# Memory keys and values from plain float32 products of the weights as loaded, the values with the memory tokens on the partitions

## Chip, cores and metric

The kernel runs on one core of one Trainium2 chip. The metric is the device time of one execution in microseconds (us), taken as the median of several runs. Engines are named as in the profile: PE is TensorE's matmul, PEld its weight load, DVE is VectorE, ACT is ScalarE, POOL is GpSimd, SP is SyncE, whose queue (SPq) issues the transfers.

## The reference, cut to what matters

One layer of a streaming encoder over T = 1088 rows (1024 prompt frames and 64 sample frames) with D = 1024 channels. Besides the big projection `h @ w_in` of the frames it needs keys and values of 256 memory tokens, which are outputs of their own and are read later by the cross-attention:

```python
def memory_kv(mem, g_mem, w_mem_kv):          # mem (1, 256, 1024), w_mem_kv (1024, 2048)
    kv = rmsnorm(mem, g_mem) @ w_mem_kv
    k, v = jnp.split(kv, 2, axis=-1)          # each (1, 256, 1024) -> 4 heads of 256
    return (k.reshape(b, N_MEM, N_MEM_HEADS, MEM_HEAD_DIM), v.reshape(b, N_MEM, N_MEM_HEADS, MEM_HEAD_DIM))
...
mem_k, mem_v = memory_kv(mem_prompt, g_mem[l], w_mem_kv[l])
...
q_sb, k_sb, v_sb, u_sg, v_sg, q_mem, z_gate = jnp.split(h @ w_in, cuts, axis=-1)
...
o_mem = cross_attend(q_mem, mem_k, mem_v)
```

## The kernel before, in words

All large products are made in float32r with each operand split in two: `split` (line 241) writes a rounded high part by a copy (on ACT, or on DVE where `lighter`, line 236, finds DVE's clock cheaper) and the rest by a subtraction on DVE; `mm3` (line 249) adds the products high by high, high by low and low by high. So one product of full precision is three matmul instructions, and each weight block of 128 x 512 elements costs a copy and a subtraction (`wsplit`, line 460).

The program is a list of steps in a fixed order. The first 16 (`n_mem`) belong to the memory keys and values: for each of 4 heads and for keys (`kv` = 0) and values (`kv` = 1) a pair of steps m = 0, 1 from `memkv_pair` (line 807) through `conv_pair` (line 591). A pair reads two raw weight tiles of 512 KB (`raw_load`, line 449), splits each into two `whl` tiles, and in each step adds up eight chunks of 128 input channels for 128 output channels (on the partitions) by 256 memory tokens (the columns) in one PSUM tile `pb`. ACT copies that into `mkT`. When both steps of a pair are done, `fin` (line 819) turns the pair round by four transposes on PE, DVE copies it to `mko` (the rows to be stored), and `split` writes `mhl` (of `mkT` for keys, of `mko` for values); two stores follow. Then come 36 Strassen units of seven steps each for `w_in` (`strassen_unit`, line 476), which need split forms (`XhB11a`, `XlT2b` and so on) of the normalised, transposed and scaled frames.

Those forms are made while the memory steps run. Each tile of frames `xt` is loaded (at most four ahead, `X_AHEAD`), squared and summed on ACT, scaled, transposed on PE in two groups of four, multiplied by its gain into `bt` (`gain`, line 714, DVE or four ACT instructions), and then five groups of subtractions and splits (`form_stages`, line 726) make seven forms of it. This work is put into the instruction streams by a planner that runs while the program is built: it keeps an estimated clock for each engine (`Clocks`, line 94), and between products (`breathe`, `fill`, lines 356 and 365) emits stages whose inputs it takes to be ready, as long as DVE and ACT are no more than `BACK` us (6 here, `BACKLOG_MEM`) ahead of PE. Each engine then works through its own instructions in that order. Its estimate for a float32r product of 256 columns is 0.107 us, and for a plain float32 product 0.0017 us for each column, 0.435 us for 256.

Weights are fetched by counting weight tiles ("wops"): `get_wop(i)` (line 398) forms the tiles up to `LA` = 2 beyond i and issues raw loads whose first wop lies up to `LA` + `RA` = 4 beyond i. The tiles share 40 slots in SBUF (`arena`, tag "s"), those of 2 KB share 11 (tag "u"). All loads and stores go through SP's queue in order. The input of the memory steps is prepared ahead of step 0 by `fm` (line 2057): the memory tokens are scaled, transposed, multiplied by `g_mem` and split into `MH["h"]` and `MH["l"]`.

Of the kernel before, what the change touches and what calls it, by code (L numbers as in the profile page):

```python
# [9 lines left out]
F32 = mybir.dt.float32  # L10
F32R = mybir.dt.float32r
# [4 lines left out]
P = 128  # L16
# [77 lines left out]
class Clocks:  # L94
# [43 lines left out]
    def at(self, *tiles):  # L138
        return max([self.wrote.get(x.tensor.name, (0,))[0] for x in tiles], default=0) + self.LATENCY
# [16 lines left out]
def encoder_layer(  # L156
# [14 lines left out]
    clock, at = clocks.t, clocks.at  # L171
    nc = Engines(tc.nc, clocks)
# [10 lines left out]
    def nm(s):  # L183
        cnt[0] += 1
        return f"{s}_{cnt[0]}"

    def A(shape, dt=F32, s="a"):
        return arena.tile(shape, dt, tag="s", name=nm(s), bufs=NSLOT)

    def U(shape, dt=F32, s="u"):  # L190
        return arena.tile(shape, dt, tag="u", name=nm(s), bufs=NSMALL)
# [3 lines left out]
    def PB():  # L195
        t = ps.tile([P, 1024], F32, tag="b", name=nm("pb"), bufs=3)
        banks["b"] = banks["b"][-2:] + [t]
        return t

    def PT():  # L200
        t = ps.tile([P, 512], F32, tag="t", name=nm("pt"), bufs=2)
        banks["t"] = banks["t"][-1:] + [t]
        return t

    def psum_free(tag, n=1):

        h = banks[tag]
        return clocks.done(h[n - 1]) if len(h) == (3 if tag == "b" else 2) else 0
# [27 lines left out]
    def lighter(src, n, cost_dve):  # L236

        t = at(src)
        return max(clock["dve"], t) + cost_dve < max(clock["act"], t) + 0.1 + 0.00084 * n

    def split(src, hi, lo):
        n = math.prod(list(src.shape)[1:])
        if src.space == bass.MemoryType.SB and lighter(src, n, DVE_BIAS + 0.07 + 0.00057 * n):
            nc.vector.tensor_copy(hi, src)
        else:
            act(hi, src)
        sub(lo, src, f32(hi))
# [6 lines left out]
    def tp(out, in_):  # L254
        n = in_.shape[0]
        nc.tensor.transpose(out, in_, ident[:n, :n])
# [7 lines left out]
    c_gmem, c_gpre, c_gffn, c_lng, c_lnb = [cols[:, 8 * i:8 * i + 8] for i in range(5)]  # L264
# [46 lines left out]
    def stream(*stages):  # L311
        st = list(stages)
        streams.append(st)
        return st
# [41 lines left out]
    def breathe():  # L356

        tick()
        while clock["dve"] < clock["pe"] + BACK[0] and clock["act"] < clock["pe"] + BACK[0]:
            st = ready(0)  # L360
            if st is None:
                break
            go(st)

    def fill(t):

        while clock["pe"] < t - 0.2:
            st = ready(t - 0.2)
            if st is None:
                break  # L370
            go(st)
# [16 lines left out]
    raws, wops, steps = [], [], []  # L388
# [6 lines left out]
    def get_raw(i):  # L395
        return raw_t[i]
# [33 lines left out]
    def wop(fn, *rs):  # L430

        wops.append(fn)
        for r in rs:
            first_wop.setdefault(r, len(wops) - 1)
            last_wop[r] = len(wops) - 1
        return len(wops) - 1
# [12 lines left out]
    def raw_load(srcs, nk):  # L449

        def f():
            r = A([P, nk, 256], F32, "raw")
            w = 256 // len(srcs)
            for i, s in enumerate(srcs):
                load(r[:, :, i * w:(i + 1) * w], s.rearrange("(k p) m -> p k m", p=P))
            return r
        raws.append(f)
        return len(raws) - 1
# [132 lines left out]
    def conv_pair(parts, xf, halves, evac, post=None, pre=None, kept=None, first=True, last=True):  # L591

        rs = [raw_load(srcs, nk) for srcs, nk in parts] if first else []

        def mk(i, m):
            nk = parts[i][1]

            def f():  # L600
                return wsplit(get_raw(rs[i])[:, :, m * P:(m + 1) * P], nk)
            return wop(f, rs[i])
        for m in range(2):
            ws = [mk(i, m) for i in range(len(parts))] if first else []
            K = sum(nk for _, nk in parts)

            def f(tiles, m=m, K=K):
                if not first:
                    tiles = kept[m]
                    ahead(AH_OUT[0] < 0)  # L610
                    AH_OUT[0] -= 1
                if kept is not None:
                    kept[m] = None if last else tiles
                if pre:
                    pre(m)
                for hi, chunks in enumerate(halves):
                    fill(psum_free("b"))
                    pt = PB()
                    for (t, s, out) in chunks:
                        k = 0  # L620
                        for i, (_, nk) in enumerate(parts):
                            for kk in range(nk):
                                xh, xl = xf(k, t, s)
                                if kk == 0:
                                    fill(at(tiles[i], xh, xl))
                                mm3(out(pt), tiles[i][:, 0, kk, :], tiles[i][:, 1, kk, :], xh, xl,
                                    k == 0, k == K - 1)
                                k += 1
                            if i < len(parts) - 1 or (t, s) != chunks[-1][:2]:
                                breathe()  # L630
                    evac(m, hi, pt)
                    breathe()
                    if post:
                        post(m, hi)
            steps.append((ws, f))

    def cols_of(a, b):
        return lambda pt: pt[:, a:b]
# [75 lines left out]
    def gain(out, src, g):  # L714

        n = src.shape[2]
        t = at(src)
        if max(clock["dve"], t) + 0.07 + 0.0042 * n < max(clock["act"], t) + 4 * (0.1 + 0.00084 * n) + G_BIAS:
            mul(out, src, g.unsqueeze(2).to_broadcast([P, 4, n]))
        else:  # L720
            for k in range(4):
                act(out[:, k], src[:, k], scale=g[:, k:k + 1])
# [82 lines left out]
    MH = {}  # L805

    def memkv_pair(h, kv):
        col = kv * D + h * 256
        parts = [([w_mem_kv[0, kh * 512:(kh + 1) * 512, col:col + 256]], 4) for kh in range(2)]
        st = {}  # L810

        def evac(m, hi, pt):
            if m == 0:
                st["t"] = U([P, 2, 256], F32, "mkT")
            act(st["t"][:, m, :], pt[:, :256])
            if m == 1:
                stream(("pe", lambda: max(at(st["t"]), psum_free("t")), fin))

        def fin():
            t = st["t"]  # L820
            pt = PT().rearrange("p (m d) -> p m d", m=2)
            for m in range(2):
                for dt in range(2):
                    tp(pt[:, m, dt * P:(dt + 1) * P], t[:, dt, m * P:(m + 1) * P])
            o = U([P, 2, 256], F32, "mko")
            nc.vector.tensor_copy(o, pt)
            dst = mem_v_prompt if kv else mem_k_prompt

            hl = A([P, 2, 2, 256], F32R, "mhl")
            split(o if kv else t, hl[:, 0], hl[:, 1])  # L830

            def put():
                store(dst[0, 0, :, h, :].rearrange("(m p) d -> p m d", p=P), o)
                store((memv if kv else memk)[h], f32(hl).rearrange("p s m d -> p (s m d)"))
            later(0, put, (o, hl))
        conv_pair(parts, lambda k, t, s: (MH["h"][k // 4][:, k % 4, :], MH["l"][k // 4][:, k % 4, :]),
                  [[(0, "a", cols_of(0, 256))]], evac)

    for h in range(4):
        for kv in range(2):  # L840
# [1205 lines left out]
    r = 0  # L2046
# [2 lines left out]
        load(vecs[r:r + n, :], v.rearrange("o (r p) -> (o r) p", p=P))  # L2049
        r += n  # L2050
    get_wop0()
    MH["h"] = [A([P, 4, 256], F32R, "memh") for _ in range(2)]
    MH["l"] = [A([P, 4, 256], F32R, "meml") for _ in range(2)]
    for j in range(2):
        d = {}

        def fm(j=j, d=d):
            bt = A([P, 8, P], F32, "bt")
            for k, p in tr4(d):
                gain(bt[:, k], p, c_gmem[:, k])  # L2060
            for q in range(2):
                split(bt[:, 4 * q:4 * q + 4], MH["h"][q][:, :, j * P:(j + 1) * P],
                      MH["l"][q][:, :, j * P:(j + 1) * P])
            READY["mem"] = READY.get("mem", 0) + 1
        stream(rms_stage(lambda j=j: mt[j], d), scale_stage(lambda d=d: d if "r" in d else None),
               ("pe", lambda d=d: max(at(d["x"]), psum_free("t")) if "cols" in READY else None, fm))
    until(lambda: not any(st[0][0] == "act" for st in streams))
    pt = PT()
# [7 lines left out]
    for n, i in enumerate([0, 1, 2, 3, 8, 4, 5, 6, 7]):  # L2076
        def ld(i=i):
            H[i] = load_tile(i, x_prompt[0], x_sample[0])
        d = {}
        e1, n1, a = rms_stage(lambda i=i: H[i], d)  # L2080
# [122 lines left out]
```

## Time and profile before

| | |
|---|---|
| median of 3 runs | 2271.82 us (2271.15 to 2273.85) |
| the profiled execution | 2273.61 us |
| its span, first to last instruction | 2271.9 us |
| mean granted TensorE clock | 0.993 |
| PE busy | 2217.8 us (98%), 16465 instructions |
| DVE busy | 1545.8 us (68%) |
| ACT busy | 760.8 us (33%) |

The span is what the trace shows; the execution's own time is 1.7 us more, and that execution was 1.8 us over the median. Busy PE counts the time from a matmul's start to its modelled end, and consecutive matmuls overlap, so the start times of a run of matmuls tell more than their durations. The lines of the views carry the line number 84 throughout, since every operation is recorded by one helper: instructions are told apart by the names of their tiles.

### The profile page before, as it was taken

To read this page: it belongs to the slowest core of one execution; us is meant where nothing else is said; L and a number is where in the kernel's file an instruction comes from. 1 tells how busy PE (TensorE), PEld (TensorE's weight loads), DVE (VectorE), ACT (ScalarE), POOL (GpSimd) and SP (SyncE) were. 2 spreads that over 40 slices of the span, in tenths; PEclk is the share of its full clock that TensorE was granted. 3 is DMA by queue.
4 is the path that set the end of the run, shared out by engine and by line. 5 is a ranking of instruction groups with operands and counts; after the bars stand their busy time and mean duration, and the time that the engine had idled before them with its cause. 6 is when DMAs were issued, how large, how long until landed. Compare 5 with 4: busy or idle time off the path is not lost. (4 is left out here: it accounts for less than half of the span.)

```text
span 2271.9 us, 40720 instructions
## 1 busy us (share of the span) xinstructions
PE 2217.8 (98%) x16465; PEld 2146.1 (94%) x16465; DVE 1545.8 (68%) x2451; ACT 760.8 (33%) x1403; POOL 61.5 (3%) x144
## 2 busy tenths in 40 slices
PE   7899999999999999999999999998999999999998
PEld 6799999999999999889999999997999999998876
DVE  7955688865777776788734353468677677675677
ACT  8442222232212232566522021354112112134353
POOL 1000000000000000011000000000000000000000
PEclk9999999999999999999999999998999999999999
DMA  6523355775476658886835252132232233257235
GB/s 209 186 87 105 125 208 199 235 224 161 167 263 215 221 188 267 295 295 219 278 127 164 88 165 68 55 105 85 86 118 92 75 118 95 72 180 261 84 112 185
DMA packets 288367, 368.27 MB, mean 162 GB/s; under 512 B 20628, under 2 KB 220404, under 8 KB 288180
## 3 DMA queue, kind: packets, MB, share of 16 engines
q1 hardware_dynamic: 288180, 365.67, 48.6%
q8 instruction: 130, 2.13, 0.4%
q14 instruction: 57, 0.47, 0.1%
HBM read 234.86 MB, written 131.80 MB: 161 GB/s over the span
## 5 line engine op out<-in xcount | busy, mean ns | idle before, releaser
L84 ACT ACTIVATE whl<-raw 128x512 fp32r<-128x512 f32 x256 | 157.8, 634 | 523.5 <-PE pb L84 203.8
L84 DVE TENSOR_TENSOR c<-pb,u 128x544 f32<-128x544 f32 (+2 forms) x236 | 168.3, 713 | 228.3 <-PE pb L84 215.6
L84 PE MATMUL pb<-fop,fop 128*128 128x512 f32 x924 | 219.3, 390 | 1.8 <-DVE p L84 1.6
L84 PEld LDWEIGHTS pb<-fop,fop 128*128 128x128 f32 x924 | 173.0, 188 | 40.5 <-DVE p L84 2.4
L84 DVE TENSOR_TENSOR whl<-raw,whl 128x512 fp32r<-128x512 f32 x270 | 180.5, 683 | 13.9 <-ACT whl L84 13.3
L84 DVE TENSOR_TENSOR u<-pb,u 128x544 f32<-128x544 f32 (+2 forms) x177 | 125.7, 710 | 58.7 <-PE pb L84 57.9
L84 DVE TENSOR_TENSOR whl<-u,whl 128x512 fp32r<-128x512 f32 x232 | 160.1, 690 | 6.1
L84 PE MATMUL pb<-XhB11a,whl 128*128 128x288 f32 x592 | 130.8, 296 | 0.7 <-ACT whl L84 0.5
L84 PE MATMUL pb<-XhB21a,whl 128*128 128x288 f32 x592 | 130.8, 296 | 0.0
L84 PE MATMUL pb<-XhB22a,whl 128*128 128x288 f32 x592 | 130.1, 295 | 0.0
L84 PE MATMUL pb<-XhB11b,whl 128*128 128x256 f32 x592 | 120.0, 286 | 0.0
L84 ACT ACTIVATE c<-c 128x1088 f32<-128x1088 f32 x38 | 42.4, 1116 | 229.8 <-DVE c L84 229.8
L84 PE MATMUL pb<-XhB21b,whl 128*128 128x256 f32 x592 | 119.1, 284 | 0.0
L84 PE MATMUL pb<-XhB22b,whl 128*128 128x256 f32 x592 | 118.6, 283 | 0.0
L84 PE MATMUL pb<-XhT2a,whl 128*128 128x288 f32 x464 | 104.4, 300 | 2.3 <-DVE whl L84 0.4
L84 PE MATMUL pb<-Xrh,whl 128*128 128x288 f32 (+1 forms) x512 | 101.4, 293 | 1.9 <-ACT ysq L84 1.9
L84 PE MATMUL pb<-XhT1a,whl 128*128 128x288 f32 x464 | 102.0, 295 | 0.9 <-DVE sgo L84 0.9
L84 PE MATMUL pb<-XhT3a,whl 128*128 128x288 f32 x464 | 102.2, 296 | 0.0
L84 PE MATMUL pb<-XhT4a,whl 128*128 128x288 f32 x464 | 102.0, 295 | 0.0
L84 PEld LDWEIGHTS pb<-XhB11a,whl 128*128 128x128 f32 x592 | 99.0, 188 | 1.1 <-ACT whl L84 0.7
L84 PEld LDWEIGHTS pb<-XhB21a,whl 128*128 128x128 f32 x592 | 99.0, 188 | 0.0
L84 PEld LDWEIGHTS pb<-XhB22a,whl 128*128 128x128 f32 x592 | 99.0, 188 | 0.0
(327 smaller groups left out, 6226.6 us busy)
## 6 DMA issues: line engine op xcount, KB each, us to landing
raw<-in_w_in_dram SPq DMA_DIRECT2D x72, 512.0 KB
raw<-in_w_ffn_in_dram SPq DMA_DIRECT2D x88, 256.0 KB
gsc<-c SPq DMA_DIRECT2D x24, 544.0 KB
grow<-gsc SPq DMA_DIRECT2D x24, 544.0 KB
raw<-in_w_branch_dram SPq DMA_DIRECT2D x24, 512.0 KB
fS<-fsum SPq DMA_DIRECT2D x44, 256.0 KB
fw<-in_w_ffn_out_dram SPq DMA_DIRECT2D x44, 256.0 KB
fa<-fS SPq DMA_DIRECT2D x44, 256.0 KB
```

What stands on the lines that cost most here:

```text
L84: r = fn(*a, **k)
```

## The change

The weights of the memory steps are no longer split. A step takes the raw tiles as they were loaded and makes eight plain float32 matmuls with the float32 tokens `MH["x"]`, which `fm` now writes directly by `gain`. For keys the weights are the stationary operand as before; for values the tokens are, so that the result has the tokens on its partitions, and `fin` needs neither transposes nor the copy to `mko` for them. The weight tiles counted by `wop` are now the raw tiles themselves, two for a pair, both with step m = 0.

```diff
     def memkv_pair(h, kv):
         col = kv * D + h * 256
-        parts = [([w_mem_kv[0, kh * 512:(kh + 1) * 512, col:col + 256]], 4) for kh in range(2)]
+        rs = [raw_load([w_mem_kv[0, kh * 512:(kh + 1) * 512, col:col + 256]], 4) for kh in range(2)]
         st = {}
+        def step(m):
+            def f(tiles):
+                w = tiles or st["w"]
+                st["w"] = w
+                fill(psum_free("b"))
+                pt = PB()
+                for kh in range(2):
+                    fill(at(w[kh], MH["x"][kh]))
+                    for k in range(4):
+                        products(pt, w[kh], MH["x"][kh], m, k, kh == k == 0, kh == 1 and k == 3)
+                    breathe()
+                evac(m, 0, pt)
+                breathe()
+                if m == 1:
+                    del st["w"]
+            steps.append(([wop(lambda r=r: get_raw(r), r) for r in rs] if m == 0 else [], f))
+
+        def products(pt, w, x, m, k, start, stop):
+            a, b = (x, w) if kv else (w, x)
+            nc.tensor.matmul(pt[:, :256], lhsT=a[:, k, m * P:(m + 1) * P], rhs=b[:, k, :], start=start, stop=stop)
 
         def evac(m, hi, pt):
...
             if m == 1:
-                stream(("pe", lambda: max(at(st["t"]), psum_free("t")), fin))
+                stream(("dve", lambda: at(st["t"]), fin) if kv else
+                       ("pe", lambda: max(at(st["t"]), psum_free("t")), fin))
 
         def fin():
-            t = st["t"]
-            pt = PT().rearrange("p (m d) -> p m d", m=2)
-            for m in range(2):
-                for dt in range(2):
-                    tp(pt[:, m, dt * P:(dt + 1) * P], t[:, dt, m * P:(m + 1) * P])
-            o = U([P, 2, 256], F32, "mko")
-            nc.vector.tensor_copy(o, pt)
+            t = o = st["t"]
+            if not kv:
+                pt = PT().rearrange("p (m d) -> p m d", m=2)
+                for m in range(2):
+                    for dt in range(2):
+                        tp(pt[:, m, dt * P:(dt + 1) * P], t[:, dt, m * P:(m + 1) * P])
+                o = U([P, 2, 256], F32, "mko")
+                nc.vector.tensor_copy(o, pt)
             dst = mem_v_prompt if kv else mem_k_prompt
...
-        conv_pair(parts, lambda k, t, s: (MH["h"][k // 4][:, k % 4, :], MH["l"][k // 4][:, k % 4, :]),
-                  [[(0, "a", cols_of(0, 256))]], evac)
+        for m in range(2):
+            step(m)
...
-    MH["h"] = [A([P, 4, 256], F32R, "memh") for _ in range(2)]
-    MH["l"] = [A([P, 4, 256], F32R, "meml") for _ in range(2)]
+    MH["x"] = [A([P, 4, 256], F32, "memx") for _ in range(2)]
     for j in range(2):
         d = {}
 
         def fm(j=j, d=d):
-            bt = A([P, 8, P], F32, "bt")
             for k, p in tr4(d):
-                gain(bt[:, k], p, c_gmem[:, k])
-            for q in range(2):
-                split(bt[:, 4 * q:4 * q + 4], MH["h"][q][:, :, j * P:(j + 1) * P],
-                      MH["l"][q][:, :, j * P:(j + 1) * P])
+                gain(MH["x"][k.start // 4][:, :, j * P:(j + 1) * P], p, c_gmem[:, k])
```

## Rows read from the trace of the kernel before

**Rows 1.** The page: busy tenths of PE in 40 equal slices of the span.
```profile
PE   7899999999999999999999999998999999999998
```

**Rows 2.** Busy time by stretch: PE, PEld, DVE, ACT, POOL; then granted clock, DMA share, GB/s.
```profile
0.00:94.00 94.00, 70.82 (x503) 66.19 (x503) 75.67 (x147) 66.57 (x157) 8.54 (x17) 0.96 0.63 203
14.00:40.00 26.00, 24.39 (x179) 23.42 (x180) 18.57 (x36) 23.80 (x53) 4.67 (x7) 1.00 0.89 286
40.00:94.00 54.00, 42.27 (x310) 39.53 (x309) 51.03 (x98) 35.24 (x94) 1.59 (x2) 0.94 0.48 154
110.00:2271.00 2161.00, 2131.53 (x15847) 2065.06 (x15846) 1455.42 (x2280) 688.79 (x1235) 52.94 (x127) 0.99 0.49 160
```

**Rows 3.** Waits of PE, 14 to 94 us: total, times, longest.
```profile
PE pb L84 <- DVE whl L84: 8.0, 8, 2.5
PE pt L84 <- ACT bt L84: 4.2, 6, 1.3
PE pb L84 <- ACT whl L84: 2.9, 2, 2.4
```

**Rows 4.** PE in order of time, memory steps: start, duration, what, count.
```profile
14.17 0.58 PE L84 MATMUL pb<-memh,whl 128*128 128x256 f32 x1 [2.41 <-ACT whl L84]
...
17.75 0.41 PE L84 MATMUL pb<-meml,whl 128*128 128x256 f32 x1
...
19.87 0.40 PE L84 MATMUL pb<-memh,whl 128*128 128x256 f32 x2
...
24.98 0.28 PE L84 MATMUL pb<-meml,whl 128*128 128x256 f32 x1
...
27.13 0.28 PE L84 MATMUL pb<-meml,whl 128*128 128x256 f32 x1
...
27.37 1.04 PE L84 MATMUL pt<-ident,xt 128*128 128x128 f32 x8
28.16 0.36 PE L84 MATMUL pb<-memh,whl 128*128 128x256 f32 x1
28.36 0.28 PE L84 MATMUL pb<-meml,whl 128*128 128x256 f32 x1
...
93.61 0.40 PE L84 MATMUL pb<-XhB11a,whl 128*128 128x288 f32 x1 [0.46 <-ACT whl L84]
```

**Rows 5.** By tile, a memory load, plain products: durations min/median/max ns, first and last start.
```profile
L84 PEld LDWEIGHTS pb<-memh,whl x256: 186/192/337, 14.2 to 92.8; 128*128 128x128 f32 x128
...
L84 PEld LDWEIGHTS pb<-wsT,vct x128: 186/192/192, 641.2 to 693.6; 128*128 128x128 f32 x128
...
L84 PE MATMUL pb<-ys,sel x4: 590/592/592, 2171.3 to 2172.6; 128*128 128x512 f32 x4
```

**Rows 6.** PE in order of time around two of those products.
```profile
641.34 1.95 PE L84 MATMUL pb<-wsT,vct 128*128 128x128 f32 x16
643.22 0.43 PE L84 MATMUL pt<-wsT,vct 64*128 64x64 f32 x2
```

**Rows 7.** DVE by group, 0 to 94 us: count, busy us, mean ns, idle before.
```profile
L84 DVE TENSOR_TENSOR whl<-raw,whl 128x512 fp32r<-128x512 f32 x33 | 21.2, 686 | 1.5 <-ACT whl L84 1.4
...
L84 DVE COPY mko<-pt 128x512 f32<-128x512 f32 x6 | 4.1, 683 | 0.0
```

**Rows 8.** ACT by group, 0 to 94 us.
```profile
L84 ACT ACTIVATE whl<-raw 128x512 fp32r<-128x512 f32 x31 | 18.6, 666 | 8.5 <-DMA raw<-in_w_mem_kv_dram 5.1 <-PE pb L84 1.5 <-DMA raw<-in_w_in_dram 1.3
```

**Rows 9.** SP's queue in order of time, and its longest wait up to 110 us.
```profile
74.92 0.39 SPq L84 DMA_DIRECT2D out_dram<-mko  x1
...
SPq L84 <- DVE mko L84: 31.8, 7, 14.8
```

**Rows 10.** DVE and ACT in order of time before the first memory product.
```profile
11.80 1.14 ACT L84 ACTIVATE bt<-pt,cols 128x128 f32<-128x128 f32 x4 [0.60 <-PE pt L84]
12.11 0.69 DVE L84 TENSOR_TENSOR bt<-pt,cols 128x512 f32<-128x512 f32 x1
```

**Rows 11.** The longest total of PE's waits, 94 to 112 us.
```profile
PE pb L84 <- DVE whl L84: 0.6, 3, 0.2
```

## Prediction

> **What bounds the kernel now.** I began with the page. PE is busy for 98% of the span, as the table above has it, and of its 40 slices of 57 us only the first two and two others lie under nine tenths [rows 1]. So nearly everywhere TensorE sets the pace, and time can be won either by giving it less work or by removing its gaps, most of which lie at the start, where the memory steps are.
>
> Busy time by stretch shows two regimes there [rows 2]. From 14 to 40 us PE is busy for 24.4 of 26 us. From 40 to 94 us it has 42.3 of 54, while DVE has 51.0 of 54: there DVE is the bound, and PE runs behind it. Beyond 110 us PE has 2131.5 of 2161 us, so a start that is earlier by some time should move the end by nearly as much.
>
> PE's waits in this stretch name the work that is late [rows 3]: 8.0 us for `whl` subtractions on DVE, 2.9 for `whl` copies on ACT (2.4 of that ahead of the first product at 14.17), and 4.2 for frame tiles (`bt`) that still hold PSUM. The subtractions queue on DVE behind frame forms that the first Strassen unit needs only after 93.6 us. PE in order of time then gives the length of the stage: from 14.17 to 93.61, when the first `w_in` product starts, it takes 79.4 us [rows 4].
>
> What does it contain? At full clock seven `meml` products start between 24.98 and 27.13, eighteen products apart, so 0.119 us for each [rows 4]. There are 4 x 2 x 2 x 8 x 3 = 384, which is 45.9 us. Eight frame transposes take from 27.37 to 28.16, 0.099 each [rows 4]: 64 of them and 8 small ones are about 6.9 us, and 28 transposes of `mkT` in the stage at the same price 2.8. That is 55.6 us. The other 23.8 are the recorded waits (8.0 + 0.5 + 4.2 = 12.7), stretches at half speed, and small gaps at each change of step. Half speed shows in the starts: from 17.75 to 19.87 ten products take 2.12, 0.212 each [rows 4], and those before are as slow. (The column of the granted clock says 1.00 for 14 to 40 us all the same, and 0.94 for 40 to 94 [rows 2]; I go by the starts.)
>
> **The change, part by part.**
>
> *Products.* 384 float32r products become 128 plain float32 ones of 256 columns. The trace has none of that width, but it has plain products of 128 and 512 columns. The 64 products of full `vct` tiles (eight for each of eight channel tiles) stand as 128 records, and the two of `ys` as four, so each instruction is run as two records [rows 5]. Sixteen such records of 128 columns take from 641.34 to 643.22, 0.1175 us each [rows 6]; the four of 512 columns start between 2171.3 and 2172.6, 0.433 us apart [rows 5]. Linear between these, 256 columns cost 0.223 us a record, 0.446 a product, and 128 products 57.1 us. That is 11.2 us more than now: by PE's work alone the change is a loss. Bounds: 0.213 a record (half of the 0.427 that 512 columns would take without any gap) gives 54.5 us; 0.223 plus a whole uncovered weight load of 0.192 [rows 5] gives 106 us. I take the interpolation, since the records of 128 columns already start closer together (0.1175) than one weight load lasts, so loads are covered there, and a wider product covers more.
>
> A rule of the Trainium skill speaks against the change here. TensorE: Matmul & The Clock Gate, under "Weight-path perf modes", says that the fast weight load is on only where the input isn't float32. The trace doesn't bear it out as a cost: plain loads last 186 to 192 ns, and the float32r loads of the memory steps have the same minimum and median [rows 5]. By the rows the products cost 57.1 us; if every load were exposed, 106.
>
> *Splits removed.* The memory stage forms 32 `whl` tiles. DVE loses 32 subtractions of 0.686, 22.0 us, four `meml` subtractions of the same shape (2.7) and four copies to `mko` for values at 0.683 (2.7) [rows 7], with a few casts some 29 us. ACT loses about 30 copies of 0.666 [rows 8], 20 us. Of DVE's 75.7 us up to 94 [rows 2] some 47 remain, of ACT's 66.6 about 46. Neither then needs the stage's 70 or more us of PE work, and no memory product waits for either except through PSUM: ACT still copies each result, with three PSUM tiles to cover its backlog of up to 6 us by two steps of 3.6 us. So the recorded 8.5 us of `whl` waits go, and PE becomes the bound of the stage.
>
> *Transposes removed.* 16 for values at 0.1 us: 1.6 us off PE.
>
> *Start.* After the last `gain` (12.80 on DVE, 12.94 on ACT) the casts and `meml` subtractions of now go [rows 10]; the first product can start at about 13.0 and not 14.17. The two raw tiles it needs are asked for first, as before.
>
> *Transfers.* No bytes change. A pair now counts two wops and not four, so raw loads are issued two pairs ahead and not one; at the beginning six raw tiles stand in SP's queue ahead of the first frames where there were four. 286 GB/s at a DMA share of 0.89 [rows 2] is some 321 at a full one, by which that 1 MB delays the frames by 3.3 us. I cost it at nothing: DVE and ACT now have some 25 us to spare in the stage, which covers it; without this cover the transposes of the first frames would hold PE by that much. A raw load now waits for PE to finish with a slot, where it waited for a `whl` split; the store of `mko` that held SP's queue until 74.92 [rows 9] comes for keys alone, behind a DVE with less to do.
>
> *Sum.* From 13.0: products 57.1, frame transposes 6.9, `mkT` of keys 1.6. At the beginning PE goes at half speed from 14.17 to 19.87 [rows 4], 2.9 us lost; I keep that, and none of the later slow stretches, since they followed the gaps. Small gaps: behind the transposes the first product starts at 28.16 and the second at 28.36, 0.20 later and not 0.119 [rows 4]; 0.08 at each of some 25 changes (16 steps, nine frame tiles) make 2.0. The frame waits of 4.2 [rows 3] had an ACT that was nearly full at the time; I take half, 2.1, with 0 and 4.2 as ends. The first `w_in` product then starts at 13.0 + 57.1 + 6.9 + 1.6 + 2.9 + 2.0 + 2.1 = 85.6, against 93.61: 8.0 us. Right behind that 0.6 us of waits for `whl` on DVE [rows 11] go as well, since DVE has no backlog there. Gain 8.6 us. The profiled execution took 2273.6 us, which makes 2265.0; it was 1.8 over the median, so I forecast 2263.2 for the median.
>
> **Rivals.**
>
> *PE with no gap.* With no frame wait, and no time at half speed, the stage ends at 13.0 + 54.5 + 8.5 + 2.0 = 78.0, a gain of 15.6 + 0.6: 2256. Against it: the slow start is there now, and transposes still wait for ACT and DVE.
>
> *New waits in place of the old.* Late raw tiles or frames. Now one store of `mko` holds SP for 14.8 us, until 74.92 [rows 9], raw loads stand behind it, and PE's longest wait for `whl` is 2.5 us [rows 3]. With no `whl` tiles formed ahead PE feels a late raw load at once. Two or three such waits, or a PE held by the delayed frames (3 us) besides the 4.2 of now, cost 5 to 8 us: 2269 to 2272. Against it: loads are issued two pairs, 14 us, ahead.
>
> *The plain product costs more at 256 columns: slower.* The stage breaks even where the forecast gain of 8.6 us is spread over 256 records, at 0.223 + 0.034 = 0.257 us a record. A weight load exposed by only half of its 0.192 us [rows 5] would give 0.319: 24.6 us, so 2288; wholly exposed, 49 us, 2313. Against it the covered loads at 128 columns [rows 6]; for it, that 256 columns, with a weight tile read in place of the split one, aren't in the trace. The fast weight load of the page cited above would be a reason for this one, and by the rows it has a small chance.
>
> **How the numbers follow.** I give 0.60 to the forecast (a gain of 5 to 12 us, 2260 to 2267), 0.12 to PE with hardly a gap (12 to 16), 0.18 to new waits (gain of 0 to 5), 0.09 to a dearer product, and 0.01 to anything else. A change of 0.2%, 4.5 us, is about what a measurement of this kernel can tell from none. The first two cases are faster by more; of the new waits I put a third (0.06) past a gain of 4.5 us; so faster 0.78, same 0.13, slower 0.09. The range runs from just above the floor of the gapless case, 2257, to new waits that eat all of the gain, 2272; only a dearer product and the far end of the gapless case lie outside.
>
> **What the changed profile would show.** Right: 256 records `pb<-raw,memx` and `pb<-memx,raw` some 0.223 us apart at full clock; no `whl` before the first Strassen unit; DVE clearly below full from 40 us on, PE above 95%; the first `XhB11a` product near 86 us; everything after it as before but earlier. Wrong: records further apart than 0.25; PE waits on `raw` transfers or on `bt`; or a first `w_in` product near 86 whose gain is lost again later, which would show as new waits past 110 us.

## The result, and the profile after

The changed kernel takes 2260.43 us (median of 4 runs, 2258.97 to 2260.93) against 2271.59 us (2271.15 to 2273.85, 4 runs) for the kernel before: a ratio of 0.9942, 95% interval 0.993 to 0.9954. The forecast was 2263.2 us, a gain of 8.6 us. The medians give 11.2 us; the ratio on record is not their quotient (which is 0.9951) and stands for 13.2. The profiled execution took 2258.97 us with a span of 2257.3 us; it was 1.5 us under its median where that of before was 1.8 over, so spans compared directly (14.6 us) say some 3 us too much.

Busy tenths of PE in 40 slices, of the page (as [rows 1]): the second slice has filled.

```profile
PE   8999999999999999999999999998999999999998
```

Busy time by stretch, in the columns of [rows 2]:

```profile
0.00:94.00 94.00, 82.97 (x449) 73.11 (x450) 64.37 (x126) 53.08 (x122) 8.26 (x17) 0.98 0.72 238
14.00:40.00 26.00, 26.00 (x144) 22.74 (x143) 14.40 (x29) 16.43 (x32) 4.32 (x6) 1.00 1.02 351
40.00:94.00 54.00, 50.57 (x283) 45.21 (x282) 45.87 (x88) 31.91 (x85) 1.66 (x3) 0.97 0.57 183
```

From 40 to 94 us PE is busy for 50.6 of 54 us where it had 42.3, and DVE for 45.9 where it had 51.0; that already holds 11 us of the first Strassen units. Up to 94 us DVE does 64.4 us of work and not 75.7.

Waits of PE up to 94 us (as [rows 3]; that for `vecs` at the very beginning left out):

```profile
PE pt L84 <- DVE mko L84: 2.7, 1, 2.7
PE pt L84 <- ACT bt L84: 0.4, 1, 0.4
PE pt L84 <- ACT xt L84: 0.3, 1, 0.3
```

All waits for `whl` are gone; one new one, for a key copy `mko`, has come. The products by tile (as [rows 5]), then PE in order of time (as [rows 4]):

```profile
L84 PEld LDWEIGHTS pb<-memx,raw x128: 190/190/337, 11.8 to 75.2; 128*128 128x128 f32 x128
L84 PE MATMUL pb<-memx,raw x128: 379/379/792, 11.8 to 75.4; 128*128 128x256 f32 x128
```

```profile
7.95 3.93 PE L84 MATMUL pt<-ident,mt 128*128 128x128 f32 x16
11.81 7.52 PE L84 MATMUL pb<-memx,raw 128*128 128x256 f32 x32
19.16 1.89 PE L84 MATMUL pb<-raw,memx 128*128 128x256 f32 x8
...
48.93 0.66 PE L84 MATMUL pt<-ident,xt 128*128 128x128 f32 x4 [0.33 <-ACT xt L84]
52.24 0.66 PE L84 MATMUL pt<-ident,xt 128*128 128x128 f32 x4 [2.65 <-DVE mko L84]
52.73 2.87 PE L84 MATMUL pb<-memx,raw 128*128 128x256 f32 x8
55.40 1.78 PE L84 MATMUL pt<-ident,xt 128*128 128x128 f32 x8
57.02 3.62 PE L84 MATMUL pb<-memx,raw 128*128 128x256 f32 x16
...
62.20 1.04 PE L84 MATMUL pt<-ident,xt 128*128 128x128 f32 x8
63.07 5.35 PE L84 MATMUL pb<-raw,memx 128*128 128x256 f32 x24
...
68.69 7.07 PE L84 MATMUL pb<-memx,raw 128*128 128x256 f32 x32
75.60 7.07 PE L84 MATMUL pb<-raw,memx 128*128 128x256 f32 x32
...
82.86 0.38 PE L84 MATMUL pb<-XhB11a,whl 128*128 128x288 f32 x1
```

Four things are to be seen. The 64 products of each orientation (those of keys are the ones shown) stand as 128 records, two each. From 68.69 to 75.60, 32 records take 6.91 us, 0.216 each. The first product starts at 11.81, right behind the transposes of the tokens. And the first `w_in` product starts at 82.86, 10.75 us earlier than the 93.61 of [rows 4].

### The profile page after: what moved, and what is told of

It reads as the page before. It is cut to its first block, busy times and chain, and to the rows that moved or that the text cites. A ratio compares the mean times of both kernels' runs of the same rounds, so it can differ in the third digit from the quotient of the medians.

```text
span 2257.3 us, 40324 instructions
## 1 busy us (share of the span) xinstructions
PE 2213.5 (98%) x16321; PEld 2137.1 (95%) x16321; DVE 1521.0 (67%) x2407; ACT 741.5 (33%) x1356; POOL 59.5 (3%) x144
## 5 line engine op out<-in xcount | busy, mean ns | idle before, releaser
L84 ACT ACTIVATE whl<-raw 128x512 fp32r<-128x512 f32 x226 | 139.8, 629 | 505.1 <-PE pb L84 207.7
L84 PEld LDWEIGHTS pb<-fop,fop 128*128 128x128 f32 x924 | 173.0, 188 | 40.5 <-DVE p L84 2.4
L84 DVE TENSOR_TENSOR whl<-raw,whl 128x512 fp32r<-128x512 f32 x238 | 160.0, 683 | 13.7 <-ACT whl L84 13.2
```

The lines of the kernel that those rows point to most:

```text
L84: r = fn(*a, **k)
```

## Experiments

All ratios are to the kernel before on the same chip, whose median lay between 2271.6 and 2274.6 us, so ratios are compared between rows rather than medians. They are the ratios on record and not quotients of these medians; a difference of 0.001 or 0.002 between two rows is not settled by them. "First vct" is the start of the first product with a `vct` tile, some 550 us later, and shows how much of an earlier start is kept. Both marks are from one profiled execution of each kernel. The bracket is the 95% interval.

| run | first `w_in` product, us | first vct, us | median, us | ratio |
|---|---|---|---|---|
| before | 93.6 | 641.3 | | 1 |
| changed | 82.9 | 628.9 | 2260.43 | 0.9942 [0.993, 0.9954] |
| e1 plain products, old layout | 84.9 | 630.6 | 2263.7 | 0.9957 [0.9942, 0.9972] |
| e2 new layout, split products | 96.1 | 643.1 | 2273.37 | 1.0 [0.999, 1.0009] |
| e3 DVE's share of the splits kept | 89.0 | 634.4 | 2265.25 | 0.9962 [0.9947, 0.9976] |
| e4 ACT's share kept | 77.9 | 626.2 | 2258.49 | 0.9933 [0.9916, 0.9949] |
| e5 half of the products | 55.6 | 623.3 | 2254.95 | 0.9921 [0.9907, 0.9934] |
| e6 mko copied by ACT | 78.4 | 627.1 | 2258.43 | 0.9936 [0.9924, 0.9949] |
| e7 gains on DVE | 82.6 | 628.9 | 2260.55 | 0.9944 [0.9931, 0.9956] |
| e8 e6 and e7 | 82.4 | 627.6 | 2258.59 | 0.9934 [0.992, 0.9947] |
| e9 late start | 83.8 | 629.2 | 2261.41 | 0.9947 [0.9932, 0.9962] |
| e10 e6, frames six ahead | 79.8 | 625.4 | 2255.48 | 0.9919 [0.9905, 0.9934] |
| e11 both shares kept | 79.7 | 631.5 | 2263.6 | 0.9951 [0.9934, 0.9968] |
| e12 frames six ahead alone | 80.2 | 627.3 | 2258.17 | 0.9938 [0.9925, 0.9952] |

### Which part of the change: e1 and e2

e1 is the changed kernel with values oriented like keys, and with their transposes and copies:

```diff
-            a, b = (x, w) if kv else (w, x)
+            a, b = w, x
...
-            t = o = st["t"]
-            if not kv:
-                pt = PT()...
+            t = st["t"]
+            pt = PT()...
```

> Plain float32 products as in the changed kernel, but values oriented like keys: their 16 transposes and 4 copies to mko are back. Theory (the splits taken off DVE and ACT are the gain): 1.6 us more on PE and one or two more waits for a transposed copy, so 2262 us (2260.5 to 2264.5), first w_in product at 84 to 86 us. Rival (the values' layout carries the gain, since it removes the turn through PSUM): 2267 us or more, first w_in product at 89 us or later.

e2 is the kernel before with the new layout for values; a pair of value steps splits two raw tiles whole:

```diff
+                hi, lo = A([P, 4, 256], F32R, "whl"), A([P, 4, 256], F32R, "whl")
+                split(r, hi, lo)
...
+                        mm3(pt[:, :256], MH["h"][kh][:, k, sl], MH["l"][kh][:, k, sl], w[kh][0][:, k, :],
+                            w[kh][1][:, k, :], kh == k == 0, kh == 1 and k == 3)
```

> The kernel before with split float32r products throughout, only the values laid out with the tokens on the partitions (weights split in two whole tiles of 256 columns, no transposes and no mko copy for values). Theory: DVE stays the bound and loses only about 2.7 of its 76 us, so 2269 us (2267 to 2272), DVE above 90% busy from 40 to 90 us. Rival (layout carries the gain): 2264 us or less.

e1 keeps 0.0043 of the 0.0058, three quarters, and its first `w_in` product comes at 84.9: as the theory had it. (By the medians it keeps 10.9 us of 11.2.) The rest goes with the layout, about what the 1.6 us of transposes and one longer wait for a turned copy make, though the intervals of the two overlap:

```profile
PE pt L84 <- DVE mko L84: 4.7, 1, 4.7
```

e2 shows no gain: its median, 2273.37 us, is 1.2 us under that of the kernel before beside it and just above the theory's range, with a ratio of 1.0. The rival is out as far as this run goes, but the theory's reason was wrong too: DVE was to stay above 90% busy, and was at 44.4 of 54 us. PE waited all the same, for the now larger splits and, in order, for frames and turned copies, and the granted clock of the stretch was 0.84 (0.94 before, [rows 2]):

```profile
40.00:94.00 54.00, 42.69 (x297) 41.03 (x298) 44.44 (x79) 35.18 (x92) 1.66 (x3) 0.84 0.63 208
```

```profile
PE pb L84 <- DVE whl L84: 5.9, 6, 1.5
PE pt L84 <- ACT bt L84: 5.1, 1, 5.1
PE pt L84 <- DVE mko L84: 3.6, 2, 1.9
```

Since e2 also had to form splits twice as wide, it doesn't price the layout alone cleanly. It does show that the stage can wait as long with DVE at 82%.

### Load or wait: e3, e4 and e11

These put the work of the splits back without letting any product wait for it. e11 has both, e3 only the `sub` (of the raw tile with itself), e4 only the `act`:

```diff
-            steps.append(([wop(lambda r=r: get_raw(r), r) for r in rs] if m == 0 else [], f))
+            steps.append(([wop(lambda r=r: extra(get_raw(r)), r) for r in rs] if m == 0 else [], f))
+
+        def extra(r):
+            for i in range(2):
+                t = A([P, 2, 4, P], F32, "unused")
+                act(t[:, 0], r[:, :, i * P:(i + 1) * P])
+                sub(t[:, 1], r[:, :, i * P:(i + 1) * P], t[:, 0])
+            return r
```

> The changed kernel with 32 subtractions of 128 x 512 put back on DVE, as the splits had them, whose results nobody reads; memory products don't wait for them. Theory (DVE's load in this stage is the cost): 22 us more on DVE, which then has some 70 us of work up to the first w_in product and makes the frame forms late; 2264 to 2269 us, waits of PE for bt, mko or XhB/XhT tiles. Rival (only the products' own wait for their splits cost time, the load doesn't matter): 2260 to 2261.5 us.

> The changed kernel with 32 copies of 128 x 512 put back on ACT, whose results nobody reads. Theory (DVE was the bound, ACT had room in the second half of the stage): at most a few waits for bt more, 2260 to 2263 us. Rival (ACT's load counts as much as DVE's): 2264 to 2268 us.

> The changed kernel with all of the weight splits' work put back, 32 copies on ACT and 32 subtractions on DVE that wait for them, results read by nobody; the memory products do not wait for them. What the load of the splits alone costs, without the products' own wait. Theory (load on DVE delays frame forms, mko copies and the first w_in splits, and is most of what the kernel before lost): 5 to 9 us more than the changed kernel, a ratio to the kernel before of 0.9965 to 0.998, first w_in product at 88 to 93 us. Rival (the wait of the products for their splits was the cost, the load alone is covered): 0.994 to 0.9955, first w_in product before 85 us.

e3 came out inside the theory's range, at 2265.25 us (0.9962). Its waits are those that were named:

```profile
PE pt L84 <- DVE mko L84: 4.9, 3, 2.0
PE pt L84 <- ACT bt L84: 1.3, 1, 1.3
PE pt L84 <- ACT xt L84: 1.2, 2, 0.7
```

They are 4.0 us more than in the changed kernel, and behind the last two for `mko` the products were slow for a while; the last:

```profile
72.61 0.66 PE L84 MATMUL pt<-ident,xt 128*128 128x128 f32 x4 [1.99 <-DVE mko L84]
73.11 8.76 PE L84 MATMUL pb<-memx,raw 128*128 128x256 f32 x32
81.70 7.07 PE L84 MATMUL pb<-raw,memx 128*128 128x256 f32 x32
```

The 32 records from 73.11 take 8.59 us where the next 32 take 6.91. So in this run DVE's load alone moved the first `w_in` product from 82.9 to 89.0.

e4 was no slower than the changed kernel, and faster than both ranges that were put for it: ACT's 20 us cost nothing. The planner, seeing ACT busy, gave 13 gains of `bt` to DVE and not 10.

e11 goes against the theory as it was put for it: the first `w_in` product and the ratio lie where the rival had them. Busy time of e11 up to 94 us, then from 40 to 82 us the kernel before, e3 and e11:

```profile
0.00:94.00 94.00, 82.36 (x446) 71.98 (x447) 74.45 (x144) 68.54 (x160) 8.70 (x17) 1.00 0.62 210
```

```profile
40.00:82.00 42.00, 31.93 (x238) 29.69 (x238) 40.48 (x80) 29.15 (x82) 1.59 (x2) 0.95 0.32 101
40.00:82.00 42.00, 36.32 (x177) 30.18 (x176) 38.52 (x73) 28.40 (x88) 3.13 (x3) 0.92 0.66 213
40.00:82.00 42.00, 40.00 (x216) 34.65 (x215) 39.27 (x79) 34.70 (x96) 3.21 (x4) 1.00 0.48 156
```

Up to 94 us DVE does 74.5 us of work and ACT 68.5, nearly what they did before (75.7 and 66.6, [rows 2]), though 14 us of the Strassen units are in that. From 40 to 82 us DVE is busy for 39.3 of 42 us and was for 40.5, but PE for 40.0 and not 31.9. And yet the first `w_in` product starts at 79.7 us and not at 93.6; 9.8 us of 12.4 are kept at the first vct, and 0.0049 of 0.0058 in the ratio (0.0032 to 0.0066 by its interval). So a full DVE does not by itself make the stage long, where no product waits for a split. How a product came to wait shows in the kernel before; DVE, ACT and PE, each in order of time:

```profile
55.36 1.29 DVE L84 TENSOR_TENSOR XlT3a<-bt,XhT3a 128x512 fp32r<-128x512 f32 x2
56.57 1.28 DVE L84 TENSOR_TENSOR whl<-raw,whl 128x512 fp32r<-128x512 f32 x2
54.92 1.33 ACT L84 ACTIVATE whl<-raw 128x512 fp32r<-128x512 f32 x2
57.30 0.50 PE L84 MATMUL pb<-memh,whl 128*128 128x256 f32 x2 [1.02 <-DVE whl L84]
```

ACT has made the first of two copies by about 55.6 (half of its 1.33 us), but its subtraction starts at 56.57, behind two `XlT3a` forms that the first Strassen unit uses from 104.7 on.

What the load costs shows later, in the first Strassen units (waits of PE from 76 to 130 us):

```profile
PE pb L84 <- DVE whl L84: 2.1, 2, 1.9
PE pb L84 <- ACT XhT4a L84: 1.0, 1, 1.0
PE pb L84 <- DVE XlT4a L84: 0.7, 1, 0.7
```

Those 3.8 us, the loss of 2.6 us against the changed kernel at the first vct, and the ratio's difference of 0.0009, 2 us, put the load at some 2 to 4 us; e3's 0.0020 says 4.5, and its first vct 5.5. These differences lie within the intervals. e3 has less work than e11 and loses more, so where the planner then puts the work counts too; no run separates that. And no run puts the wait back without the load.

### Is PE now the bound: e5

```diff
-                    for k in range(4):
-                        products(pt, w[kh], MH["x"][kh], m, k, kh == k == 0, kh == 1 and k == 3)
+                    for k in range(2):
+                        products(pt, w[kh], MH["x"][kh], m, k, kh == k == 0, kh == 1 and k == 1)
```

> The changed kernel with only half of the memory products (two of four chunks of each weight tile; the other half of the sum is left out), 64 in place of 128, so 27.6 us less on PE at the 0.216 us a record that the changed kernel shows; loads, frame forms and stores are untouched. Theory (PE is now the bound of the stage): the first w_in product moves up from 82.9 us by at least 8 us and at most 27.6, up to where DVE's 46 us of frame forms and the arrival of the frames hold it; 2240 to 2253 us. Rival (frames, transfers or DVE already set the length of the stage, PE merely fits in): first w_in product moves up by less than 3 us, 2258 to 2261 us.

e5 leaves out half of the sum in every key and value. The first `w_in` product moved up by 27.3 us, all that was left out, as the theory allowed; the time, 2254.95 us, lies between the two ranges, for by the first vct only 5.6 us of it remained, and 0.0021 in the ratio, 4.8 us. The rest went into waits, here of PE from 8 to 110 us:

```profile
PE pt L84 <- DVE mko L84: 4.8, 1, 4.8
PE pt L84 <- DVE bt L84: 4.6, 2, 4.4
PE pb L84 <- DVE XlT3b L84: 2.4, 1, 2.4
PE pb L84 <- DVE whl L84: 1.8, 1, 1.8
```

So in the changed kernel PE does set the pace, but the frame forms follow about 5 us behind it, and the start of the first `w_in` product is not by itself the measure of the gain.

### What is left: e6, e7, e8, e10 and e12

e6 copies `mko` on ACT (`act(o, pt)` in place of `nc.vector.tensor_copy(o, pt)`). e7 replaces `G_BIAS` = 1 by 4 in `gain` up to the end of the memory steps, so that gains go to DVE; e8 has both. e10 is e6 with `X_AHEAD = 6`, e12 the changed kernel with `X_AHEAD = 6`.

> The changed kernel with the copy from PSUM to mko for keys on ACT and not on DVE. In the changed kernel PE stands 2.7 us for one such copy that queues on DVE behind frame forms, and goes at half speed for eight products after it, about 1 us. Theory: this wait is real and costs what it shows; without it 2257 to 2259 us, first w_in product at 79 to 81 us. Rival (the wait only moves, since ACT's queue is as long there): 2260 us.

> The changed kernel with the planner's choice between one DVE instruction and four on ACT for the gain of a frame tile pushed to DVE while the memory steps run. In the run with copies kept on ACT the planner did the same of its own accord (13 gains on DVE where the changed kernel has 10), and the first w_in product came at 77.9 us. Theory (the long ACT gains hold PSUM and with it PE's transposes): first w_in product at 78 to 81 us, 2256 to 2259 us. Rival (that early start came from the order of the streams by chance): 2259.5 to 2262 us.

> Both edits: the mko copy of keys on ACT, the gains of frames on DVE. Theory: PE without gaps up to the first w_in product at 77.5 to 79 us, and 2255.5 to 2258 us, not the sum of the two gains since both remove the same gaps. Rival: DVE's queue then delays the frame forms, and what is won ahead of the first w_in product is lost in the first Strassen units, 2259 to 2262 us.

> The changed kernel with the mko copy of keys on ACT and frame tiles loaded up to six ahead and not four. With half of the products left out only about 5 us were won, so the frame forms follow closely behind PE. Theory (the arrival of the frames holds the forms back): fewer waits of PE for whl and forms in the first Strassen units, 1 to 3 us less than with the mko copy on ACT alone, a ratio to the kernel before of 0.992 to 0.9932. Rival (DVE's work itself is what follows behind, or six frames ahead hold slots that weights need): a ratio of 0.9933 or more.

> The changed kernel with frame tiles loaded up to six ahead and nothing else; the mko copy of keys stays on DVE. Theory (the arrival of the frames was what held back the forms behind PE): a ratio of 0.992 to 0.993 to the kernel before, close to the run with both edits (0.9919), the wait for mko smaller since DVE has its forms done earlier. Rival (the two edits are needed together, since the mko wait remains): 0.9935 to 0.9945, with a wait of PE for mko of 2 us or more.

e6 took away the wait for `mko`, and its first `w_in` product came 4.5 us earlier, at 78.4; but at once PE waited 2.4 us for a `whl` on DVE, and 1.8 us remained at the first vct. The time, 2258.43 us, is the theory's, but the ratio, 0.9936, can't be told from 0.9942. e7 gained nothing: PE stood once for 3.8 us for an `rstd` (the scale of a frame) that queued on DVE. So the early start of e4 was no merit of the DVE gains alone. e8 got its first `w_in` product at 82.4, not the 77.5 to 79 that were expected, with a single wait for `bt` of 2.9 us; its 2258.59 us lies between the two ranges (its 0.9934 would be 2256.6 beside the 2271.59 of the result, inside the theory's), and not for the theory's reason.

e10 is the best version run that leaves nothing out, 0.9919 [0.9905, 0.9934], 2255.48 us, just past the near end of the theory's range: it is faster than the kernel before by 15 to 22 us, and by some 5 us than the changed one, though the two intervals touch at 0.9930 to 0.9934. PE has no wait but this one between 8 and 110 us:

```profile
PE pt L84 <- ACT bt L84: 2.1, 4, 0.8
```

e12 answers to neither side: the ratio, 0.9938, is the rival's, but the wait for `mko`, which the rival needed, is gone (the largest is 1.1 us, for `xt`). Whether e10's two edits add up to more than either is not settled by these intervals.

### The start: e9

```diff
+            bt = A([P, 8, P], F32, "bt")
             for k, p in tr4(d):
-                gain(MH["x"][k.start // 4][:, :, j * P:(j + 1) * P], p, c_gmem[:, k])
+                gain(bt[:, k], p, c_gmem[:, k])
+            for q in range(2):
+                hi, lo = A([P, 4, P], F32R, "memh"), A([P, 4, P], F32R, "meml")
+                split(bt[:, 4 * q:4 * q + 4], hi, lo)
+                add(MH["x"][q][:, :, j * P:(j + 1) * P], f32(hi), f32(lo))
```

> The changed kernel with the memory tokens split and put together again (a copy, a subtraction and an addition for each of four pieces) ahead of the first product, so that PE stands idle between the transposes of the tokens and the first product as it did in the kernel before. Theory (in the changed kernel the first products come right behind the transposes, and that both starts the stage earlier and ends PE's half speed early): first product near 15 us and not 11.8, starts of the records twice as far apart (0.43) for some 3 to 6 us, first w_in product at 86 to 90 us, and 2262 to 2267 us. Rival (the slow start belongs to a fixed time, or to the kind of product, and not to the gap): first product near 15 us, the records 0.22 apart from the beginning or within 1 us, first w_in product at 84 to 86 us, 2260 to 2263 us.

PE of e9 in order of time:

```profile
7.59 3.93 PE L84 MATMUL pt<-ident,mt 128*128 128x128 f32 x16
15.04 9.35 PE L84 MATMUL pb<-memx,raw 128*128 128x256 f32 x32 [3.52 <-DVE memx L84]
24.23 1.89 PE L84 MATMUL pb<-raw,memx 128*128 128x256 f32 x8
```

The first 32 records take 9.19 us, where the changed kernel takes 7.35 and 32 records at full speed 6.91: 2.3 us lost, which at half speed is some 4.6 us of slow products, against 0.4 us lost without the gap. In the other runs without the gap 0.1 us (e4, e6, e7) to 1.2 (e8) are lost in the same way, so the gap stands clear of that spread. That is the theory's side. The first `w_in` product, at 83.8, is nearest to the rival's 84 to 86, and the time, 2261.41 us (0.9947, 1 us over the changed kernel, within the intervals), is the rival's. Against e6, which has no `mko` wait either, e9 starts its first `w_in` product 5.4 us later; 2.1 of that are left at the first vct, and 0.0011 in the ratio. The slow start is shown; that it costs its full length at the end is not, for the reason that e5 gave.

## Why the prediction was right

The time lay inside the range, and the mechanism is in the main the one forecast: dearer products, but no wait for splits. By its steps:

- *Products dearer on PE, the stage shorter all the same.* Right. 128 products cost 256 x 0.216 = 55.3 us where the float32r ones cost 45.9; the forecast was 57.1. The straight line between 128 and 512 columns put 7 ns too much on a record; 0.216 is nearer to the lower bound of 0.213. The rival of exposed weight loads is out: loads still last 190 ns and the records start 0.216 apart. By the rule of the Trainium skill (TensorE: Matmul & The Clock Gate, "Weight-path perf modes") these float32 weights get no fast load. The trace shows no product held up by a load, and not which loads were fast ones.
- *No product waits for a split.* Right, and by e11, which keeps the earlier start and the values' layout too, this is the larger part of the gain; e3 puts more on the load. The sentence "there DVE is the bound, and PE runs behind it" was wrong in part, though: with DVE as busy, PE in e11 was done with the stage 13.9 us earlier (79.7 against 93.6). In the lines from 54.92 to 57.30 above it held PE by the order of its queue. Its remaining work was mis-sized as well: up to the first `w_in` product DVE has 54.5 us and not 47, and the planner gave it 14 gains where it had nine. From 40 to 82.86 us DVE is busy for 36.0 of 42.9 us and PE for 39.4, 92%, so the sign "PE above 95%" was missed.
- *Start.* Forecast 13.0, measured 11.81. The first half of a product needs only the first half of the channels, so it starts before the last gain (11.91 on DVE); the four gains were all on DVE.
- *Half speed at the beginning.* Mis-sized most: 2.9 us were kept from the kernel before, but 0.44 are lost (7.35 against 6.91 for 32 records). e9 shows why: the long slow start belonged to the gap ahead of the first product. A second slow stretch, not forecast, came behind the `mko` wait: the eight records from 52.73 to 55.40 take 2.67 us in place of 1.73, and the eight transposes behind them 1.62 where those at 62.20 take 0.87. That makes 2.1 us in all.
- *Waits of the frames.* Forecast 2.1 us of `bt`. Measured 0.7 of `bt` and `xt`, and 2.7 of a key copy `mko` queued on DVE behind forms, a wait of the same kind as those that were removed. That the total came near was luck: the largest wait is one that was not forecast.
- *The sum up to the first `w_in` product.* 85.6 forecast, 82.86 measured: 2.7 earlier. The start makes -1.2, the products -1.8, the slow stretches -0.8 and the waits +1.3, together -2.5; the other -0.2 are transposes and small gaps. Set against the kernel before, the stage went from 79.4 us to 71.1 (11.81 to 82.86): products +9.4, transposes -1.2, recorded waits -9.3 (12.7 to 3.4), and slow stretches and small gaps together -7.3 (11.1 to 3.8). The slow stretches and small gaps were worth nearly as much as the recorded waits.
- *After it.* Forecast 0.6 us more. From the first `w_in` product to the first vct it is 547.7 us before and 546.0 after, 1.7 us; no run shows where the other 1.1 us comes from.
- *Transfers hidden.* No wait of PE for a raw tile or for a frame's load is among its waits up to 94 us. The six raw tiles ahead of the frames cost nothing that shows; e10 and e12 leave open how much earlier frames would help.

What the prediction didn't see is how near the next limit is. It treated the time of the first `w_in` product as the gain; e5 shows that, with frames loaded four ahead, only some 5 us more were to be had that way.

## What to carry to other kernels

An engine that is 95% busy in a stage needn't be its bound: ask what in its queue is needed now, and whether the engine that sets the end waits behind work that isn't. A dearer instruction that takes its operands as they were loaded can beat three cheaper ones that wait for a preparation in a shared queue. And an earlier start at one point is worth only as much as the next stream in line is ahead: follow a later mark too.

## What the runs showed of the hardware

A plain float32 product of 256 columns stands as two records, 0.216 us apart at full speed, so 0.43 us, with weight loads of 190 ns covered; the three float32r products in its place took 0.36 (0.119 each). At the beginning of the execution TensorE goes at the lower of its two levels, 1.2 GHz, by the starts (transposes of the tokens, 16 in 3.9 us with short waits in it, 0.24 each; eight frame transposes at full speed take 0.8, 0.1 each, [rows 4]): without a gap behind them the first 32 product records lose 0.44 us to it (0.1 to 1.2 over the runs), with a gap of 3.5 us they lose 2.3, while the column of the granted clock says 1.00 from 14 to 40 us (above, and [rows 2]) and for e9's slow records too. In the middle, after PE had stood 2.65 us, the same column shows 0.70 for the stretch from 52.5 to 55 us.
